# Attention's products of weights and values, both lanes side by side on TensorE: a change to the order of issue

## The chip, the cores and the metric

The kernel runs on one core of a Trainium2 chip. Five engines work side by side, each through its own instructions in a fixed order: TensorE (PE in the profile, with its weight loads as PEld), VectorE (DVE), ScalarE (ACT), GpSimd (POOL) and SyncE (SP), which here only starts transfers. The metric is the device time of one execution in microseconds (us), the median of several runs.

## The reference, cut to what matters

Two layers over 1024 latent and 256 context tokens, each with three token mixers (attention, a depthwise convolution, a Hyena long convolution), an output projection and an expert layer. The change lies in attention:

```
s = (jnp.einsum('bqhd,bkhd->bhqk', qn, k_nope, ...)
     + jnp.einsum('bqhr,bkr->bhqk', qr, k_rope, ...))
w = jax.nn.softmax(s * scale, axis=-1).astype(v.dtype)
return jnp.einsum('bhqk,bkhd->bqhd', w, v)
```

There are 8 heads. A latent query reads all 1280 keys, a context query the 256 context keys; scores contract over 96 numbers, and a head's value has 64 columns.

## The kernel before

Python code records the instructions, and a scheduler then sets each engine's order from priorities (the order of recording, unless a context says otherwise) and from its own model of the durations. What comes out is fixed at build time, so an instruction that waits holds up everything behind it on its engine.

`mla` (L595) records the attention of one layer. The work of a head is cut into units: one tile of 128 keys (kt) for two lanes of queries. For latent tokens the lanes are the two halves (512 queries each) of one head; in the first layer there are also units whose lanes are two heads' 256 context queries. A layer has 80 latent units, and the first layer 8 context units besides, so 168 units in all, with two products of weights and values each: 336.

A unit (`attend`, L772) does this for each lane. `score` (L783) multiplies keys by queries in three products, high and low parts apart (`mm3`, L93, hence lines L95 to L97), into one of the two PSUM banks tagged "s"; ScalarE takes the exponential (L788) into a tile `pt`, of which there are six. `pv` (L790) multiplies the values Vt (128 keys by 64 columns) by pt, in plain float32 through `mm` (L99, the line L100 of the profile), into PSUM tile `o`: lane 0 into partitions 0 to 63, lane 1 into 64 to 127 of the same bank. GpSimd adds each pt to a running sum (L801), from which the denominators come later (`finish`, L809: the products `p<-psum,ones`, a reciprocal on VectorE).

The loop at L672 records for unit n: the scores of unit n+1 for lane 0, a step of the next head's preparation, the scores of lane 1, another step, then `pv` of unit n, and another step. The preparation of the next head (`queries`, `keys`, `largest`) contains 24 or more products `p<-K,Q` (L757), each of which VectorE reduces to a maximum (L758) out of one of three banks "p". The long convolutions (`hyena`) are recorded within head 0 and are spread by the scheduler over the following heads. Their blocks go round: products `hx` on TensorE, two multiplications on VectorE (L862, L863), two additions on GpSimd (L864, L865), a split into two parts on ScalarE and VectorE (L90, L91), products `ha` on TensorE, each with one PSUM bank.

Of the kernel before, what the change touches and what calls it, by code (L numbers as in the profile page):

```python
# [29 lines left out]
def _bc(ap, n):  # L30
    """A DRAM row read by n partitions."""
    return bass.AP(tensor=ap.tensor, offset=ap.offset, ap=[[0, n]] + [list(x) for x in ap.ap])


def lap(parts):
    """The steps of parts one after another; what a part has left after it yields 1 alternates with the next one's first steps."""
    before = iter(())
    for part in parts:
        for late in part:
            yield  # L40
            if next(before, None):
                yield
            if late:
                break
        for _ in before:
            yield
        before = part
    for _ in before:
        yield


class Kernel:
# [9 lines left out]
    def stream(self, l, i):  # L62
        """128 tokens behind a layer's attention, or behind all of it."""
        return self.xd[l][128 * i:128 * i + 128] if i < 8 else self.xc[128 * (i - 8):128 * (i - 8) + 128]
# [5 lines left out]
    def banks(self, es, **tags):  # L70
        """PSUM banks for a part of the program, so many for each use."""
# [30 lines left out]
    def rsqrt(self, out, ss):  # L102
        """(ss + eps) ** -0.5 of a few columns."""
        n = out.shape[-1]
# [4 lines left out]
    def consts(self):  # L109
        nc, A, cp = self.nc, self.A, self.cp  # L110
# [16 lines left out]
        # the mixers' outputs: heads but the last two, the last two, the channels  # L127
# [6 lines left out]
    def mod(self, l, P, ps):  # L134
        """Two of the six rows at a time; yields between loads."""
# [31 lines left out]
    def sin(self, P, out, x, n):  # L167
        """sin of [128, n] of any size: x - 2 pi round(x / 2 pi) in parts."""
# [14 lines left out]
    def filter_mlp(self, F, P, PL, ps, taps):  # L183
        """The filter networks' last hidden layers, 64 partitions for each network, and what else the taps need."""
# [22 lines left out]
        for k, w in enumerate((w1, w2)):  # L207
# [8 lines left out]
            if k:  # L216
                # the sum and the difference of the two directions' weights, with zeros for the other network
# [9 lines left out]
    def filter_taps(self, l, F, P, ps, f):  # L227
        """Sums and differences of the two directions' taps, and the sums of their squares (twice the taps')."""
# [6 lines left out]
        for i in range(nts):  # L235
# [7 lines left out]
            if i in (0, 8):  # L243
                # no backward tap at zero
# [14 lines left out]
    def spectra(self, pools, PF, ps, jobs, lo_t, nk, units, mats, er_, n, nrm_i):  # L259
        """jobs: (taps, DRAM of the spectra); the transforms' matrices are read once for all. Pools for each job; the  # L260
        last one's is everybody's, and may come after the first yield. PF: for what is to be split."""
# [25 lines left out]
        def norms(f, rsr):  # L287
            """Two steps: the sums over the positions, then their roots as a row for all partitions."""
# [20 lines left out]
        for nm, s_, op in kinds:  # L309
            dat += [operands((nm, s_, op), ji) for ji in range(len(dat), len(J))]  # L310
            for un, ex, m, kind, unit in units:
# [15 lines left out]
                if roots:  # L327
                    # not before the first products
# [19 lines left out]
    def filters(self):  # L348
        A = self.A
        with ExitStack() as es:  # L350
# [11 lines left out]
            # kinds: real, imaginary, and the first unit's real part for the sines  # L362
# [34 lines left out]
    def win(self, l, M):  # L397
# [3 lines left out]
        with ExitStack() as es:  # L401
# [3 lines left out]
            with ExitStack() as es2:  # L405
                # first what comes before the products
# [23 lines left out]
                for g0, g1 in ((0, 4), (4, 8), (8, 10)):  # L430
# [27 lines left out]
                    # q, kv, k_rope  # L458
# [107 lines left out]
    def conv(self, l, M, P, ps):  # L566
        """Layer norm over the channels, silu."""
# [27 lines left out]
    def mla(self, l, M):  # L595
        """Attention, with the convolution's norm and the long convolutions in between: one order of TensorE's work."""
        nc, A, S, V, G = self.nc, self.A, self.S, self.V, self.G
        last = l == 1
        with ExitStack() as es:
# [13 lines left out]
            def fixed(i):  # L613
                """The rows that all heads share."""
# [12 lines left out]
            def values(i):  # L627
                """V of four heads, by tokens."""
# [12 lines left out]
            def prepare(h):  # L641
                """A head's keys and queries, and the queries' largest scores, by steps."""
# [29 lines left out]
            for h, w in enumerate(windows):  # L672
                # the next head's steps between this one's tiles of keys
# [35 lines left out]
    def queries(self, P, ps, l, h, M, Q, QC, tab):  # L709
        """A head's queries."""  # L710
# [27 lines left out]
    def keys(self, P, ps, l, h, M, K):  # L738
        """A head's keys."""
# [8 lines left out]
    def largest(self, P, ps, K, Q, nq, k0, nk, first):  # L748
        """The negated largest score of each query, into its row 96."""
# [22 lines left out]
    def attend(self, P, ps, l, lanes, Vt, kts):  # L772
        """Two lanes (head, keys, queries, the first of so many queries, their place) side by side, by tiles of keys."""
# [5 lines left out]
        def unit(n, kt):  # L779
# [3 lines left out]
            def score(i):  # L783
                _, K, Q, c, _, _ = lanes[i]
                p = ps("s")
                self.mm3(p[:, :N], K[0][:, s], K[1][:, s], Q[0][:, c:c + N], Q[1][:, c:c + N], True, True)
# [3 lines left out]
            def pv():  # L790
                if n == 0:
                    st.o = ps("o")
                for i, pt in enumerate(u.pts):
                    c = 64 * (lanes[i][0] % 4)
                    self.mm(st.o[64 * i:64 * i + 64, :N], Vt[kt][:, c:c + 64], pt[:, :N], n == 0, kt == kts[-1])
# [29 lines left out]
    def heads(self, l, h, M):  # L825
        """The weights of a head's keys and queries."""
# [6 lines left out]
    def hyena(self, l, M, P, ps):  # L833
        """Yields where other work may come first."""
# [11 lines left out]
        def table(src):  # L846
            """A matrix in two parts, each [128, a, b]."""
# [8 lines left out]
        def product(px, gt, u, w, y):  # L856
            """(Xc | Xs) in PSUM times the filter's spectrum (real, imaginary), in two parts."""
# [19 lines left out]
        def halves(o, blk):  # L877
            """Even and odd parts, folded once more: one block of their transforms, and back."""
# [52 lines left out]
        def whole(o, ct, D):  # L931
            """The odd multiples, the sum, and the gate."""
# [39 lines left out]
        def context(o):  # L972
            T = self.t(P, [128, 2, 2, 256], F32R, "hT", bufs=2)
            # C2 S2 C4 and S4 C2i S2i
# [22 lines left out]
            for u, ic, is_ in ((0, 4, 5), (1, 2, 3)):  # L997
                yh, yl = y[u]
                # the even unit's cosines and the odd unit's sines are symmetric
# [19 lines left out]
        def parts(o):  # L1019
            # halves folded about their middles; the operands of the sines of odd multiples (e, oe) run backwards, by which  # L1020
            # their transform is the cosines' up to signs, which the spectra carry
# [17 lines left out]
    def wout(self, l, R):  # L1039
# [4 lines left out]
        with ExitStack() as es:  # L1044
            # first the places that attention leaves early
# [30 lines left out]
            def source(n):  # L1076
                """n columns of the mixers' outputs: the last heads' part comes last."""
# [36 lines left out]
            def channels(i):  # L1114
                """The convolutions' part of a tile of tokens."""
# [14 lines left out]
            def heads(i):  # L1130
                """The heads' part, the residual, norm 2, and the router."""
# [73 lines left out]
    def affinities(self, R, s):  # L1205
        """Softmax over the experts (s: 0 latent, 1 context)."""
# [13 lines left out]
    def selected(self, R, s):  # L1220
        """The right-hand sides of the compaction: token, token, affinity in two parts."""
# [8 lines left out]
    def route_ctx(self, R, ps, ar, wk):  # L1230
        """Each expert's tokens of the context: the places of the 32 largest."""
# [19 lines left out]
    def route(self, R, ps, tag, P):  # L1251
        """Each expert's 128 tokens: rows of 128 affinities (tile of tokens, expert) are sorted and merged by twos to the 128th largest."""
# [5 lines left out]
        def merge(x, y, out, n, steps):  # L1258
            """n rows of bitonic sequences, descending."""
# [9 lines left out]
        for r in range(8):  # L1269
            # two halves in turns  # L1270
# [8 lines left out]
        for n in (64, 32):  # L1279
            # the 128 largest of two sorted rows, and those sorted  # L1280
# [10 lines left out]
        # all above the 128th largest, and the first of those equal to it  # L1291
# [22 lines left out]
    def moe(self, l, R):  # L1314
        nc, A, S, V, G = self.nc, self.A, self.S, self.V, self.G
        last = l == 1
        with ExitStack() as es:
            PA = self.pool(es, f"moa{l}", 1)
            if last:
                PM = self.pool(es, f"mob{l}", 1)  # L1320
                # the output projection leaves this place first
# [3 lines left out]
                # where nothing of the output projection's is  # L1325
# [10 lines left out]
            def fetch(e):  # L1336
                """The expert's tokens and gates; its tokens' rows."""
# [41 lines left out]
            def tokens(e):  # L1379
                """Its tokens, features by partitions."""  # L1380
# [28 lines left out]
            def weights(nm, e, kh, after=None):  # L1409
                w = large()  # L1410
                if after is not None:
                    # the load follows what is in the queue already
                    V.tensor_copy(w[:, 0, 0:1], after)
# [3 lines left out]
            def product(w, kh, x, accs, early=0):  # L1417
                """accs += x's tokens by half of the rows."""
# [12 lines left out]
            def up(e, kh, m):  # L1431
# [7 lines left out]
                # the first parts while VectorE chooses  # L1439
# [77 lines left out]
            def norm(x, g):  # L1517
                """The final norm of 128 tokens in place."""
# [5 lines left out]
            def final():  # L1524
                """All tokens as though the last expert had none, then its own."""
# [15 lines left out]
            # the first expert's weights come in while the experts choose  # L1541
# [9 lines left out]
            for e in range(17):  # L1551
                if e == 0:
                    # not before what the choice waits for
# [34 lines left out]
    def run(self, stop=None):  # L1588
# [9 lines left out]
        for l in range(2):  # L1598
            # the second layer's from the other end: what the first leaves early comes first
            self.side = ("left", "right")[l]  # L1600
            with ExitStack() as es:
                MP = self.pool(es, f"mix{l}", 1)
                # first what is in use until the end
# [12 lines left out]
            with ExitStack() as es:  # L1616
# [3 lines left out]
                # sums over an expert's rows, all and earlier ones  # L1620
# [12 lines left out]
def _r12(a):  # L1633
    """float64 -> the nearest float32 with 12 significant bits."""
# [10 lines left out]
def _mat(a):  # L1645
    """[t, f] -> [128, 2, t / 128, f]: both parts, rows by partition."""
# [4 lines left out]
def _constants():  # L1651
# [14 lines left out]
    # rotary tables  # L1666
# [131 lines left out]
```

## Time and profile before

| | us |
|---|---|
| median of 3 runs (lowest, highest) | 3534.89 (3531.77, 3535.91) |
| profiled execution, its span from the first to the last instruction | 3541.2 |
| TensorE busy in it | 3291.5 (93%) |
| VectorE, ScalarE, GpSimd busy | 2533.4 (72%), 1692.6 (48%), 1296.5 (37%) |
| attention of the first layer, from 540 to 1040 | 500 |
| attention of the second layer, from 2265 to 2755 | 490 |

The profile gives no time of the profiled execution other than its span, which is 6.3 us above the median of the runs. How to read it: a product in plain float32 is recorded as two MATMULs with a weight load each, so that the 336 products of weights and values are 672 records. Ends of matmuls are modelled and overlap the next one's start; what a product costs TensorE is therefore read from start to start. "128*64 128x512" is a matmul with 128 rows and 64 columns of weights and 512 columns streamed.

### The profile page before, as it was taken

The numbers are of one execution on the slowest core, as the hardware profiler recorded it, in microseconds if no ns is written. First come the engines' busy times: TensorE is split into PE (matmuls) and PEld (weight loads), VectorE is DVE, ScalarE is ACT, GpSimd is POOL, SyncE is SP. The second block draws the span as 40 slices with busy tenths as digits, with TensorE's granted clock in tenths as the row PEclk, the third lists the DMA queues.
The fourth block names the chain that finished last, engine by engine and source line by source line (L and its number), as shares of the span: only waits on it lengthen the run. The fifth ranks groups of instructions, "written<-read, shape, count | busy, mean of one in ns | idle before, by whom it ended". The sixth has DMA issues, their size and how long they took to land. (4 is left out here: it accounts for less than half of the span.)

```text
span 3541.2 us, 42696 instructions
## 1 busy us (share of the span) xinstructions
PE 3291.5 (93%) x15595; PEld 2244.1 (63%) x15595; DVE 2533.4 (72%) x3507; ACT 1692.6 (48%) x2447; POOL 1296.5 (37%) x1130
## 2 busy tenths in 40 slices
PE   8898989999999699999999879899999959999996
PEld 2467864566448566766767567646554647888885
DVE  7744796676557767777777556966663668999886
ACT  4214334333433256556665443433333426777775
POOL 4421434644553421112211113464455423343334
PEclk9898989999999799999999989899999979999998
DMA  8871121131234467777777611211222457999994
GB/s 314 309 248 62 38 90 40 49 93 47 60 113 140 158 253 276 297 276 282 295 271 297 211 59 54 84 50 49 67 73 80 155 220 289 374 382 378 373 380 181
DMA packets 138075, 660.80 MB, mean 187 GB/s; under 512 B 20520, under 2 KB 58824, under 8 KB 107145
## 3 DMA queue, kind: packets, MB, share of 16 engines
q1 hardware_dynamic: 112681, 582.85, 43.8%
q0 software_dynamic: 24768, 74.05, 7.6%
q8 instruction: 123, 2.02, 0.2%
q10 hardware_dynamic: 416, 1.18, 0.1%
q14 instruction: 87, 0.71, 0.1%
HBM read 589.24 MB, written 68.78 MB: 186 GB/s over the span
## 5 line engine op out<-in xcount | busy, mean ns | idle before, releaser
L91 DVE TENSOR_TENSOR mwl<-raw,mwh 128x1024 fp32r<-128x1024 f32 x710 | 881.2, 1277 | 225.4 <-ACT mwh L90 215.8
L90 ACT ACTIVATE mwh<-raw 128x1024 fp32r<-128x1024 f32 x768 | 791.1, 1057 | 353.4 <-PE acc L97 117.5
L96 PE MATMUL acc<-mwl,xh 128*128 128x512 f32 x1024 | 406.5, 397 | 0.5 <-DVE mwl L91 0.5
L97 PE MATMUL acc<-mwh,xl 128*128 128x512 f32 x1024 | 404.1, 396 | 0.1
L801 POOL TENSOR_TENSOR psum<-psum,pt 128x512 f32<-128x512 f32 x252 | 328.6, 1312 | 185.7 <-ACT pt L788 179.7
L788 ACT ACTIVATE pt<-s 128x512 f32<-128x512 f32 (+1 forms) x336 | 196.6, 586 | 390.8 <-PE s L97 363.5
L95 PE MATMUL acc<-mwh,xh 128*128 128x512 f32 x1024 | 373.9, 402 | 6.3 <-ACT xh L90 5.9
L100 PE MATMUL o<-pt,Vt 128*64 128x512 f32 (+1 forms) x672 | 338.9, 607 | 0.4 <-ACT ao L805 0.3
L758 DVE TENSOR_REDUCE mx<-p 128x1 f32<-128x512 f32 (+1 forms) x374 | 209.0, 587 | 153.4 <-PE p L100 152.6
L1498 POOL DMA_INDIRECT xd<-ymoe,idx x31 | 104.4, 3367 | 549.2 <-DVE ymoe L1494 472.6
L95 PEld LDWEIGHTS acc<-mwh,xh 128*128 128x128 f32 x1024 | 192.7, 190 | 69.4 <-ACT mwh L90 10.5
L96 PEld LDWEIGHTS acc<-mwl,xh 128*128 128x128 f32 x1024 | 194.1, 190 | 44.5 <-DVE mwl L91 2.6
L97 PEld LDWEIGHTS acc<-mwh,xl 128*128 128x128 f32 x1024 | 193.4, 190 | 40.1 <-issue 0.8
L91 POOL TENSOR_TENSOR mwl<-raw,mwh 128x1024 fp32r<-128x1024 f32 x58 | 150.4, 2598 | 185.2 <-ACT mwh L90 121.5
L564 DVE SCALAR_TENSOR_TENSOR cacc<-pad,cw,cacc 128x1295 f32<-128x1295 f32 (+1 forms) x90 | 165.7, 1841 | 1.3
L97 PE MATMUL mm<-hTh,wfl 128*128 128x512 f32 (+1 forms) x400 | 151.2, 379 | 12.7 <-DVE wfl L91 12.7
L95 PE MATMUL mm<-hTh,wfh 128*128 128x512 f32 (+1 forms) x400 | 152.5, 381 | 4.0 <-ACT wfh L90 4.0
L96 PE MATMUL mm<-hTl,wfh 128*128 128x512 f32 (+1 forms) x400 | 152.0, 380 | 0.0
L562 POOL TENSOR_TENSOR cacc<-cacc,tap 128x1295 f32<-128x1295 f32 (+1 forms) x30 | 97.0, 3233 | 120.8 <-ACT tap L561 118.6
L100 PEld LDWEIGHTS o<-pt,Vt 128*64 128x64 f32 x672 | 62.0, 134 | 110.2 <-issue 104.2
L100 PE MATMUL cx<-raw,xcT 128*32 128x512 f32 x1024 | 122.9, 597 | 0.0
L95 PE MATMUL mm<-woh,yhh 128*128 128x512 f32 x280 | 115.7, 416 | 6.0 <-ACT wt L1126 3.9
(539 smaller groups left out, 7322.4 us busy)
## 6 DMA issues: line engine op xcount, KB each, us to landing
raw<-in_w_gate_dram SPq DMA_DIRECT2D x64, 2048.0 KB
raw<-in_w_up_dram SPq DMA_DIRECT2D x64, 2048.0 KB
raw<-in_w_down_dram SPq DMA_DIRECT2D x64, 2048.0 KB
mw<-in_mod_w_dram SPq DMA_DIRECT2D x48, 1024.0 KB
ht<-in_k_C_dram POOLq DMA_DIRECT2D x24, 512.0 KB, 4.9
wfr<-in_w_fm_dram SPq DMA_DIRECT2D x20, 512.0 KB
hd<-h SPq DMA_DIRECT2D x18, 512.0 KB
fw<-in_k_filt_dram POOLq DMA_DIRECT2D x17, 512.0 KB, 6.2
```

Of the source, the lines that this page charges most:

```text
L90: self.S.activation(hi, src, AF.Copy)
L91: (eng or self.V).tensor_tensor(lo, src, hi.bitcast(F32), ALU.subtract)
L95: mm(out, ah, bh, start=first, stop=False, skip_group_check=True)
L96: mm(out, ah, bl, start=False, stop=False, skip_group_check=True)
L97: return mm(out, al, bh, start=False, stop=last, skip_group_check=True)
L100: return self.T.matmul(out, a, b, start=first, stop=last, skip_group_check=True)
L562: G.tensor_tensor(a, a, t, ALU.add)
L564: V.scalar_tensor_tensor(a, x, w2[:, ct, k:k + 1], a, ALU.mult, ALU.add)
L758: V.tensor_reduce(mx[:, q, n:n + 1], p[:, :N], AX.X, ALU.max)
L788: S.activation(pt[:, :N], p[:, :N], AF.Exp, scale=ATT_SCALE)
L801: (V if tail and n > 8 else G).tensor_tensor(sm[:, :N], st.sums[i][:, :N], pt[:, :N], ALU.add)
L1498: G.indirect_dma_start(self.xd[l], bass.IndirectOffsetOnAxis(ap=d["idx"], axis=0), y, None, compute_op=ALU.add)
```

## The change

In `pv` the two products are recorded under a higher priority, and are not to be issued before the last product that the latest `score` recorded, which is lane 1 of the next unit. `score` keeps that product for it. Nothing is added or removed; what is computed stays the same. The diff also drops comments and docstrings of the whole file, which do not reach the program, and lines behind L794 move by two (L801 becomes L803, for instance).

```
             def score(i):
                 _, K, Q, c, _, _ = lanes[i]
                 p = ps("s")
-                self.mm3(p[:, :N], K[0][:, s], K[1][:, s], Q[0][:, c:c + N], Q[1][:, c:c + N], True, True)
+                self.scored = self.mm3(p[:, :N], K[0][:, s], K[1][:, s], Q[0][:, c:c + N], Q[1][:, c:c + N], True, True)
                 pt = u.pts[i] = self.t(P, [128, 512], F32, "pt", bufs=6)
                 S.activation(pt[:, :N], p[:, :N], AF.Exp, scale=ATT_SCALE)
 
             def pv():
                 if n == 0:
                     st.o = ps("o")
-                for i, pt in enumerate(u.pts):
-                    c = 64 * (lanes[i][0] % 4)
-                    self.mm(st.o[64 * i:64 * i + 64, :N], Vt[kt][:, c:c + 64], pt[:, :N], n == 0, kt == kts[-1])
+                with self.tc.high_priority(400), self.tc.issue_after(self.scored.ins):
+                    for i, pt in enumerate(u.pts):
+                        c = 64 * (lanes[i][0] % 4)
+                        self.mm(st.o[64 * i:64 * i + 64, :N], Vt[kt][:, c:c + 64], pt[:, :N], n == 0, kt == kts[-1])
```

The first place is TensorE in the middle of the second layer's seventh head, before the change. Here s are scores, o the products of weights and values (two lanes of one tile have the same Vt), p the next head's products for the largest scores.

```order
L95 MATMUL s_21512<-Q0h_17870,K0h_17872 128x512
L96 MATMUL s_21512<-Q0l_17871,K0h_17872 128x512
L97 MATMUL s_21512<-Q0h_17870,K0l_17873 128x512
L100 MATMUL o_21351<-pt_21491,Vt_4560_20567 64x512
L100 MATMUL p_21453<-K1h_17876,Q1h_17874 128x512
L100 MATMUL p_21456<-K1h_17876,Q1h_17874 128x512
L95 MATMUL s_21524<-Q0h_17870,K0h_17872 128x512
L96 MATMUL s_21524<-Q0l_17871,K0h_17872 128x512
L97 MATMUL s_21524<-Q0h_17870,K0l_17873 128x512
L100 MATMUL o_21351<-pt_21500,Vt_4560_20567 64x512
```

The same place after the change:

```order
L95 MATMUL s_21512<-Q0h_17870,K0h_17872 128x512
L96 MATMUL s_21512<-Q0l_17871,K0h_17872 128x512
L97 MATMUL s_21512<-Q0h_17870,K0l_17873 128x512
L95 MATMUL s_21524<-Q0h_17870,K0h_17872 128x512
L96 MATMUL s_21524<-Q0l_17871,K0h_17872 128x512
L97 MATMUL s_21524<-Q0h_17870,K0l_17873 128x512
L100 MATMUL o_21351<-pt_21491,Vt_4560_20567 64x512
L100 MATMUL o_21351<-pt_21500,Vt_4560_20567 64x512
L100 MATMUL p_21465<-K1h_17876,Q1h_17874 128x512
L100 MATMUL p_21474<-K1h_17876,Q1h_17874 128x512
```

The o of lane 0 has moved behind the scores of the next tile's lane 1 and stands beside the o of lane 1; p products follow the pair or stand between the two lanes' scores.

The second place is TensorE at the first unit of the first layer, before the change. hx and ha here are transposes of the convolutions.

```order
L97 MATMUL s_3849<-Q0h_3582,K0l_3585 128x512
L100 MATMUL o_3918<-pt_3841,Vt_681_3683 64x512
L586 MATMUL hx_4267<-ident_60,m1y_4265 128x128 x2
L574 MATMUL ha_4277<-ident_60,cacc_1771 128x128 x2
L95 MATMUL s_3903<-Q0h_3582,K0h_3584 128x512
L96 MATMUL s_3903<-Q0l_3583,K0h_3584 128x512
L97 MATMUL s_3903<-Q0h_3582,K0l_3585 128x512
L100 MATMUL o_3918<-pt_3847,Vt_681_3683 64x512
```

The same place after the change:

```order
L97 MATMUL s_3849<-Q0h_3582,K0l_3585 128x512
L586 MATMUL hx_4267<-ident_60,m1y_4265 128x128 x2
L574 MATMUL ha_4277<-ident_60,cacc_1771 128x128 x2
L95 MATMUL s_3903<-Q0h_3582,K0h_3584 128x512
L96 MATMUL s_3903<-Q0l_3583,K0h_3584 128x512
L97 MATMUL s_3903<-Q0h_3582,K0l_3585 128x512
L100 MATMUL o_3918<-pt_3841,Vt_681_3683 64x512
L100 MATMUL o_3918<-pt_3847,Vt_681_3683 64x512
```

The convolutions' instructions now follow the scores directly, with no o ahead of them. Over the whole program TensorE's order before has 293 products of 512 columns that stand alone, 12 pairs and one row of three; after, 8 alone and 156 pairs (four of them as two rows of four). Of the 16 products of 256 columns, all stood alone; after, 4 do, and 6 pairs. On the other engines 515 of 3356 rows of VectorE, 388 of 2352 of ScalarE, 99 of 1131 of GpSimd and 19 of 640 of SyncE change their place, all of them in the two attention stages or at their edges; the other stages keep their order.

## Rows read from the trace of the kernel before

**Rows 1.** Busy time of the engines in four stretches: us, busy (count), PEclk.

```profile
core 0: us, PE busy (x) PEld busy (x) DVE busy (x) ACT busy (x) POOL busy (x), PEclk, DMA share, GB/s
540.00:1040.00 500.00, 489.48 (x2015) 266.95 (x2015) 318.19 (x527) 189.01 (x366) 262.96 (x255) 1.00 0.21 59
2040.00:2265.00 225.00, 194.54 (x859) 157.33 (x859) 159.15 (x200) 90.94 (x157) 67.63 (x59) 0.91 0.17 55
2265.00:2755.00 490.00, 480.83 (x1874) 257.51 (x1871) 302.43 (x494) 181.34 (x347) 260.10 (x254) 0.99 0.22 67
```

**Rows 2.** Groups by line, 540 to 1040: count, busy, mean ns, idle before it and releasers.

```profile
L801 POOL TENSOR_TENSOR psum<-psum,pt 128x512 f32<-128x512 f32 x126 | 164.7, 1316 | 87.3 <-ACT pt L788 82.4 <-DVE wql L91 3.4
L758 DVE TENSOR_REDUCE mx<-p 128x1 f32<-128x512 f32 (+1 forms) x182 | 100.9, 580 | 84.3 <-PE p L100 83.8
L788 ACT ACTIVATE pt<-s 128x512 f32<-128x512 f32 (+1 forms) x172 | 98.7, 577 | 190.9 <-PE s L97 171.8 <-PE o L100 15.4 <-POOL psum L801 2.6
```

**Rows 3.** The products o: all records of the tile.

```profile
L100 PE MATMUL o<-pt,Vt x672: 379/593/644, 534.5 to 2751.9; 128*64 128x512 f32 x160, 128*64 128x256 f32 x8
```

**Rows 4.** TensorE in order of time, second layer's last head: start, us, what.

```profile
2728.88 0.50 PE L95 MATMUL s<-Q1h,K1h 128*128 128x512 f32 x1
2729.22 0.39 PE L96 MATMUL s<-Q1l,K1h 128*128 128x512 f32 x1
2729.45 0.40 PE L97 MATMUL s<-Q1h,K1l 128*128 128x512 f32 x1
2729.77 1.07 PE L100 MATMUL o<-pt,Vt 128*64 128x512 f32 x2
2730.78 0.50 PE L95 MATMUL s<-Q1h,K1h 128*128 128x512 f32 x1
```

**Rows 5.** TensorE in order of time, where two o stand next to each other.

```profile
2567.61 0.39 PE L96 MATMUL s<-Q0l,K0h 128*128 128x512 f32 x1
2567.85 0.39 PE L97 MATMUL s<-Q0h,K0l 128*128 128x512 f32 x1
2568.16 1.08 PE L100 MATMUL o<-pt,Vt 128*64 128x512 f32 x4
2569.17 0.39 PE L95 MATMUL hx<-hT,ht 128*128 128x256 f32 x1
2569.40 0.28 PE L96 MATMUL hx<-hT,ht 128*128 128x256 f32 x1
2569.51 0.28 PE L97 MATMUL hx<-hT,ht 128*128 128x256 f32 x1
```

**Rows 6.** TensorE in order of time, an o of 256 columns.

```profile
1000.33 0.65 PE L100 MATMUL o<-pt,Vt 128*64 128x256 f32 x2
1000.91 0.50 PE L95 MATMUL s<-Q1h,K1h 128*128 128x512 f32 x1
1001.25 0.39 PE L96 MATMUL s<-Q1l,K1h 128*128 128x512 f32 x1
```

**Rows 7.** Weight loads at the pair of rows 5, and single ones by line, 2265 to 2755.

```profile
2568.16 0.20 PEld L100 LDWEIGHTS o<-pt,Vt 128*64 128x64 f32 x4 [0.36 <-issue]
...
L100 PEld LDWEIGHTS o<-pt,Vt 128*64 128x64 f32 x320 | 29.7, 134 | 53.7 <-issue 52.4 <-ACT pt L788 0.2
```

**Rows 8.** Stretches of 25 us in which VectorE is fullest.

```profile
590.00:615.00 25.00, 24.62 (x84) 10.62 (x83) 21.17 (x36) 10.73 (x21) 8.73 (x7) 1.00 0.18 48
2340.00:2365.00 25.00, 25.00 (x92) 11.80 (x91) 22.61 (x34) 11.05 (x21) 14.04 (x11) 1.00 0.14 39
```

**Rows 9.** The convolutions' additions on GpSimd by line, 540 to 1040, then 2265 to 2755.

```profile
L864 POOL TENSOR_TENSOR m1y<-m1y,m2y 128x128 f32<-128x128 f32 (+1 forms) x28 | 19.0, 678 | 52.0 <-DVE m2y L863 44.9 <-DVE m L761 4.2 <-ACT Q1h L769 1.9
...
L864 POOL TENSOR_TENSOR m1y<-m1y,m2y 128x128 f32<-128x128 f32 (+1 forms) x24 | 13.4, 559 | 47.7 <-DVE m2y L863 45.0 <-DVE m L762 2.5
```

**Rows 10.** GpSimd's sums in the last head, in order of time.

```profile
2728.79 1.28 POOL L801 TENSOR_TENSOR psum<-psum,pt 128x512 f32<-128x512 f32 x1 [0.61 <-ACT pt L788]
2730.68 1.28 POOL L801 TENSOR_TENSOR psum<-psum,pt 128x512 f32<-128x512 f32 x1 [0.61 <-ACT pt L788]
```

## The prediction

> **What bounds the kernel now.** I read first the busy time by stage. In the two attention stages, 990 us together, TensorE is busy 489.48 of 500 and 480.83 of 490 us, at a granted clock of 1.00 and 0.99, while VectorE has 318.19 and 302.43, GpSimd 262.96 and 260.10, ScalarE 189.01 and 181.34 us [rows 1]. The groups by line then say whom the others wait for: VectorE's maxima stand idle 83.8 us for TensorE's p, ScalarE's exponentials 171.8 us for the scores, and GpSimd's sums 82.4 us for those exponentials [rows 2]. So everybody waits for TensorE, and a microsecond less of work there is a microsecond less of time until another engine, or a round trip through several, comes to the front. The other stages keep their order, and I leave them as they are.
>
> Busy time of TensorE has modelled, overlapping ends, so next I read starts in order of time. In the last head, where nothing stands between, one lane takes 2730.78 - 2728.88 = 1.90 us: three scores and one o [rows 4]. Scores follow each other at 0.235 us (2567.61 to 2567.85 [rows 5], 2729.22 to 2729.45 [rows 4]), so three are 0.705 and one lone o costs 1.90 - 0.705 = 1.19 us: 1.01 until the next product starts, some 0.09 more ahead of it (0.32 from the last score, not 0.235), and 0.10 behind it (the first score after it takes 0.34).
>
> **What a pair costs.** The kernel before has a few places where the two lanes' products already stand next to each other, and one of them shows the price. From the last score at 2567.85 to the second hx at 2569.40 are 1.55 us [rows 5]. The score's own 0.235 and one hx of 256 columns at 0.12 (2569.40 to 2569.51, rounded) off, the block of two products, four records, is 1.19 us: as much as one alone. The two lanes write different halves of the partitions and run at the same time. The trace has 11 such rows of four, the first at 594.5 and the last at 2708.4, all with 1.01 us from their first start to the next product's; this one stands for them.
>
> **A rule against it.** The row shows four weight loads in 0.20 us, 0.13 us each when alone [rows 7], so those of lane 1 are hidden beside those of lane 0. The Trainium skill, page "TensorE: Matmul & The Clock Gate", section "Part 3: Packing small matmuls — row/col tiling", says that a weight load overlaps products in flight only when the row group differs; here the two lanes share all rows and differ in columns, so by that rule the second lane's two loads of 0.134 us would be exposed. Here the trace disagrees with it. What that would make of the time is a rival below, with a small chance.
>
> **The change part by part.** It adds and removes no instruction. (1) *Products of 512 columns.* In the order before, 293 stand alone, 12 in pairs and three in a row, which is 293 + 12 + 2 = 307 slots for the 320 products; after, 8 alone and 156 pairs are 164 slots. 143 slots fewer at 1.19 us: 170.2 us. (2) *Products of 256 columns.* 16 slots become 10. One costs 0.58 us until the next start (1000.33 to 1000.91), and with the same 0.19 around it 0.77 [rows 6]: 6 x 0.77 = 4.6 us. Together 336 products are in the order, twice as many records in the trace [rows 3]. TensorE's work in the two stages falls by 175 us, from 990 to 815.
>
> (3) *The wait that is added.* The pair waits for the scores of the next unit. Behind it on TensorE stand p, hx and the following scores. The wait for its own exponentials costs nothing: the scores ahead of the pair go into the two "s" banks, which are free only once both exponentials of the pair's own tile are done, so TensorE can't reach the pair earlier than its data. The price moves to the scores, which need those banks. A unit of the last head would take TensorE 2 x 0.705 + 1.19 = 2.60 us, and an exponential 0.58 to 0.60 [rows 2]; from the end of a lane's scores to the same bank's next use lie a pair and the other lane's scores, 1.9 us, against one exponential with its hand-over, or two when they queue (1.2 us). I cost it at nothing; that cover is gone only where ScalarE stands more than 0.7 us behind.
>
> (4) *GpSimd's sums and the six pt.* A sum is 1.28 us [rows 10], two per unit 2.56. Against 1.90 us per lane now, GpSimd waits 0.61 each time; in the last heads it comes just level with TensorE's 2.60 and its slack is gone. Per stage it has 263 of 408 us. Bounds: 0, and 10 us for the two ends together (two heads of 10 units at up to 0.5 us each); I take 3.
>
> (5) *VectorE.* Its 621 us are 63% of 990 and 76% of 815. In its fullest stretches it has 21.2 and 22.6 of 25 us [rows 8]. A stretch of 25 us holds some 4 merged pairs, 5 us, so TensorE would want 20, and these two lose 1.2 and 2.6 us. Bounds: 0, and 15 for four times that in shorter bursts; I take 6.
>
> (6) *The convolutions' round trips.* hx, VectorE, GpSimd, ScalarE, VectorE, ha: 28 and 24 blocks [rows 9]. Where the fixed order puts a block's next product just in time, TensorE now reaches it too early, by 1.19 us for each merged pair between. Bounds: 0, where a block's slack holds it, and 52 x 1.19 = 62 us, where each block shows one pair's worth. GpSimd's waits of 44.9 and 45.0 us for VectorE within these blocks [rows 9] say that the path is long, but TensorE is almost never idle for it now. I take a third of the bound, 0.33 x 62 = 20 us, nearer to the row without stalls. (7) *Transfers.* SyncE's and GpSimd's queues keep nearly all their places, and the transfers use 0.21 and 0.22 of their engines in these stages [rows 1]: nothing.
>
> Sum: 170.2 + 4.6 - 3 - 6 - 20 = 146 us. The profiled execution's span of 3541.2 becomes 3395; it lies 6.3 us above the median of the runs, so the median of 3534.89 becomes 3389.
>
> **The rivals.** *Round trips come to light.* VectorE and the convolutions' blocks are late at nearly every turn: 62 + 15 + 10 = 87 us of the 175 are given back, and the time is 3535 - 88 = 3447 at its worst, about 3425 in its middle (110 us saved). For it speaks VectorE at 76%; against it, that it waits 83.8 us for TensorE in one stage alone [rows 2]. With it goes the clock: in the stretch before the second attention TensorE is busy 194.54 of 225 us and the clock is granted at 0.91, where attention has 1.00 [rows 1], so stalls on TensorE could cost more than their own length. *Only the products overlap.* By the rule on weight loads a pair costs 2 x 0.134 = 0.27 us more; 143 x 0.27 = 38 us less gain, 3427. Rows 5 and 7 speak against it, eleven times. *No pairing in time.* If lane 1's product, though next in the queue, started a slot later, nothing would be gained: 3535. Step 3 says why its operand is there. *Slower: the scores wait for the exponentials.* Two lanes' scores in a row take both banks at once. If ScalarE, which also splits the heads' keys and queries, were late by one slot in each unit, each of 168 units would lose 1.19 us, 200 us against the 175 gained: 3560. It decides from 175 / 168 = 1.04 us per unit. Against it: ScalarE is busy 38% of the stage, and exponentials wait for scores 171.8 us, not the other way [rows 2].
>
> **How the numbers follow.** The forecast, with part of the cover gone: chance 0.66, 3389, its own range 3362 to 3412. Round trips come to light: 0.24, 3412 to 3447. Weight loads exposed: 0.04, 3427. No cover needed at all, or a little more than 175 us gained because today's few stalls go as well: 0.02, 3355. No pairing in time: 0.02, 3535. Slower: 0.02, 3560. The range that holds 8 in 10 is 3358 to 3434. A measurement of this kernel can tell about 0.2%, 7 us, from no change. Faster has 0.66 + 0.24 + 0.04 + 0.02 = 0.96, same 0.02, slower 0.02.
>
> **What would show it.** In the profile after, o stands in rows of four records with some 1.08 us, about 160 of them, and a unit of the last head repeats every 2.6 us, not 3.8. The two attention stages last about 990 - 146 = 844 us with the granted clock still near 1.0, VectorE's share is near 74%, and the idle time of the maxima and of the exponentials behind TensorE has shrunk. The second rival shows as idle time of TensorE ahead of hx, ha or p with VectorE or ScalarE as releaser, and as a granted clock under 0.97. The prediction is wrong if rows of four take clearly over 1.1 us, if scores wait for exponentials at most units, or if a stage outside attention moves by over 10 us.

## The result, and the profile after

The changed kernel takes 3404.98 us (median of 4 runs, 3398.4 to 3407.12), the kernel before 3534.01; the ratio is 0.9629 (95% interval 0.9615 to 0.9643). That is 131 us less by the ratio, 129 by the two medians. In a later comparison it was 0.9624 (0.9608 to 0.964), 133 us less by both. The forecast was 3389, with a range from 3358 to 3434.

The two attention stages by engine, after the change. The first one again begins at 540; the second is taken 28 us ahead of its first o and to 3 us behind its last, as in [rows 1].

```profile
core 0: us, PE busy (x) PEld busy (x) DVE busy (x) ACT busy (x) POOL busy (x), PEclk, DMA share, GB/s
540.00:970.00 430.00, 409.83 (x2002) 259.49 (x2001) 311.27 (x524) 186.82 (x363) 259.05 (x252) 0.98 0.24 69
2192.00:2617.00 425.00, 405.04 (x1871) 255.03 (x1871) 302.94 (x493) 179.85 (x345) 263.94 (x253) 0.96 0.25 78
```

They last 855 us instead of 990: 135 us less, all of the result within its uncertainty. Three things are to be read against [rows 1]. TensorE is not busy for 20.17 + 19.96 = 40.1 us, where it was 10.52 + 9.17 = 19.7. The granted clock is 0.98 and 0.96, where it was 1.00 and 0.99. The other engines do the same work in less time; VectorE's share is 72%.

TensorE in the last head, in order of time, answers to [rows 4]:

```profile
2604.47 0.40 PE L97 MATMUL s<-Q1h,K1l 128*128 128x512 f32 x1
2604.79 1.08 PE L100 MATMUL o<-pt,Vt 128*64 128x512 f32 x4
2605.80 0.50 PE L95 MATMUL s<-Q1h,K1h 128*128 128x512 f32 x1
...
2607.09 0.39 PE L97 MATMUL s<-Q1h,K1l 128*128 128x512 f32 x1
2607.40 1.08 PE L100 MATMUL o<-pt,Vt 128*64 128x512 f32 x4
2608.41 0.50 PE L95 MATMUL s<-Q1h,K1h 128*128 128x512 f32 x1
```

The pair of four records takes 1.01 us until the next product's start, and a unit 2607.40 - 2604.79 = 2.61 us, where two lanes took 3.80. Among the single records behind such a row of four, lane 1's products start less than 0.01 us behind lane 0's: the two lanes do run at the same time. The weight loads at one such pair, and the products' records as a whole, answer to [rows 7] and [rows 3]:

```profile
2604.79 0.20 PEld L100 LDWEIGHTS o<-pt,Vt 128*64 128x64 f32 x4 [0.37 <-issue]
...
L100 PE MATMUL o<-pt,Vt x672: 379/593/1116, 534.2 to 2614.0; 128*64 128x512 f32 x160, 128*64 128x256 f32 x8
```

The median is the same 593 ns; the longest is 1116 where it was 644: records of that kind stand where the clock was lower, as seen below. The groups by line, from 540 to 970, answer to [rows 2]:

```profile
L803 POOL TENSOR_TENSOR psum<-psum,pt 128x512 f32<-128x512 f32 x126 | 165.2, 1330 | 32.6 <-ACT pt L788 30.6
L758 DVE TENSOR_REDUCE mx<-p 128x1 f32<-128x512 f32 (+1 forms) x182 | 98.4, 577 | 38.5 <-PE p L100 38.1
L788 ACT ACTIVATE pt<-s 128x512 f32<-128x512 f32 (+1 forms) x170 | 97.1, 577 | 129.9 <-PE s L97 96.5 <-PE o L100 17.9 <-POOL psum L803 12.4
```

Everybody still waits mostly for TensorE, but less: the maxima 38.1 us where it was 83.8. The 12.4 us behind GpSimd's sums (2.6 before) are new. In the last head GpSimd's sums stand without a gap, where [rows 10] had 0.61 us between them:

```profile
2601.20 7.69 POOL L803 TENSOR_TENSOR psum<-psum,pt 128x512 f32<-128x512 f32 x6
```

What TensorE waits for in the first attention stage (us in total, times, longest):

```profile
PE p L768 <- DVE m L762: 9.2, 6, 2.4
PE hx L95 <- DVE m2y L865: 3.9, 4, 1.6
PE hx L900 <- DVE hT L91: 3.8, 2, 3.5
PE ha L97 <- DVE yl L91: 0.9, 1, 0.9
```

L768 are the transposes of the negated maxima (m), which close a head's preparation; the others are the convolutions' blocks. All four wait for VectorE. One of these waits in order of time:

```profile
736.34 1.06 PE L900 MATMUL hx<-ident,cacc 128*128 128x128 f32 x4 [3.47 <-DVE hT L91]
737.05 0.78 PE L95 MATMUL s<-Q1h,K1h 128*128 128x512 f32 x1
737.62 0.63 PE L96 MATMUL s<-Q1l,K1h 128*128 128x512 f32 x1
738.05 0.63 PE L97 MATMUL s<-Q1h,K1l 128*128 128x512 f32 x1
738.61 1.64 PE L100 MATMUL o<-pt,Vt 128*64 128x512 f32 x4
```

and the engines around it by stretch, columns as above:

```profile
725.00:735.00 10.00, 7.76 (x34) 3.96 (x32) 10.00 (x18) 3.92 (x8) 5.30 (x5) 1.00 0.36 94
735.00:740.00 5.00, 3.67 (x11) 1.85 (x11) 5.00 (x6) 0.60 (x1) 3.00 (x3) 0.66 0.00 0
740.00:765.00 25.00, 24.50 (x146) 17.98 (x145) 17.26 (x32) 10.54 (x22) 18.50 (x18) 1.00 0.36 95
```

VectorE is busy all the time from 725 to 740. TensorE stands idle for 3.47 us, and then the granted clock goes to 0.66 on the average of 5 us: for part of it the lower of the two levels, 1.2 GHz. Scores start 0.43 us apart instead of 0.235, and a pair is recorded with 1.64 us instead of 1.08. So this wait is paid for twice. Behind the first o of each layer the changed kernel has nine waits of 1.5 us or more. During seven of them, or soon after, the lower level comes; at two, of 1.60 and 1.67 us, it does not, and an eighth stretch at the lower level follows waits of 0.21 and 0.47 us only. In the profile of the second measurement one more wait, of 1.94 us, is not followed by it. The kernel before has one such stretch there, behind waits of 1.23 and 0.47 us.

### The profile page after: what moved, and what is told of

It reads as the page before. It is cut to its first block, busy times and chain, and to the rows that moved or that the text cites. A ratio compares the mean times of both kernels' runs of the same rounds, so it can differ in the third digit from the quotient of the medians.

```text
span 3396.6 us, 42699 instructions
## 1 busy us (share of the span) xinstructions
PE 3126.6 (92%) x15595; PEld 2226.8 (66%) x15595; DVE 2532.4 (75%) x3507; ACT 1691.3 (50%) x2447; POOL 1300.8 (38%) x1130
## 5 line engine op out<-in xcount | busy, mean ns | idle before, releaser
L803 POOL TENSOR_TENSOR psum<-psum,pt 128x512 f32<-128x512 f32 x252 | 333.1, 1341 | 68.3 <-ACT pt L788 64.4
L100 PE MATMUL o<-pt,Vt 128*64 128x512 f32 (+1 forms) x672 | 184.1, 611 | 0.0
L96 PE MATMUL mm<-wol,yhh 128*128 128x512 f32 x280 | 112.1, 401 | 0.0
```

The source lines that it names most:

```text
L96: mm(out, ah, bl, start=False, stop=False, skip_group_check=True)
L100: return self.T.matmul(out, a, b, start=first, stop=last, skip_group_check=True)
L803: (V if tail and n > 8 else G).tensor_tensor(sm[:, :N], st.sums[i][:, :N], pt[:, :N], ALU.add)
```

## Experiments

"Idle" below is the time in which TensorE is not busy in the two attention stages, and "clock" is what the granted clock costs there: (1 - granted clock) times the time, added up over short stretches, since two digits over a whole stage leave some 2 us open. Of the clock's cost some 7 us lie ahead of the second layer's first o in the kernel before, and as many in the changed kernel; what falls into idle time (2 us in the changed kernel) counts in both. Stages are taken as above, from 5 or 6 us behind the first o in the first layer and from 27 to 30 us ahead of it in the second, to 3 to 5 us behind the last.

### Priority without the bond

```
-                with self.tc.high_priority(400), self.tc.issue_after(self.scored.ins):
+                with self.tc.high_priority(400):
```

> The two products of a tile keep their higher priority but not the bond to the next tile's last score. In TensorE's order 285 products of 512 columns then stand alone again (8 in the changed kernel) and 18 pairs are left. Theory (the gain comes from two lanes' products standing next to each other): the time is that of the kernel before, 3534 us, within 15. Rival (the gain comes from the priority, which makes the scheduler lay the rest of attention better): about 3405 us, as with the whole change.

Measured: 3531.38 us, ratio 0.9987 (0.9977 to 0.9997). The stages:

```profile
540.00:1040.00 500.00, 490.62 (x2021) 271.11 (x2020) 317.74 (x527) 189.44 (x367) 260.08 (x255) 1.00 0.20 59
2262.00:2752.00 490.00, 480.72 (x1874) 263.03 (x1872) 300.45 (x494) 180.70 (x347) 260.15 (x254) 0.98 0.22 68
```

They are as long as before, 990 us. The theory's time came. The priority alone does nothing that counts; with the bond to the next tile's last score (`issue_after`) come the pairs, since lane 0's product then can't be laid as soon as its pt is ready. Whether the bond would do without the priority was not run.

### Pairs in one half of the partitions

```
-                        self.mm(st.o[64 * i:64 * i + 64, :N], Vt[kt][:, c:c + 64], pt[:, :N], n == 0, kt == kts[-1])
+                        h = 64 * i if n == 0 else 0
+                        self.mm(st.o[h:h + 64, :N], Vt[kt][:, c:c + 64], pt[:, :N], n == 0, kt == kts[-1])
```

> The changed kernel, but from each window's second tile of keys on both lanes' products go into partitions 0 to 63 of the bank (lane 1's share of the output is left out, its products are still made). Order and pairs are nearly the same: some 150 pairs, about 145 of them in one half. Theory (two products overlap because they use different halves): each such pair costs some 0.97 us more, and only the 0.2 us around a block is still shared: 3490 to 3520 us, with about 2.0 us from a pair's first start to the next product. Rival (what is saved is the change between 64 and 128 columns around each block, or better order): 3400 to 3415 us.

Measured: 3508.42 us, ratio 0.9924 (0.9904 to 0.9944), as the theory had it. The stages, and TensorE in the last head:

```profile
543.00:1032.00 489.00, 468.54 (x2008) 280.19 (x2007) 311.80 (x524) 187.01 (x363) 255.62 (x253) 0.98 0.20 60
2256.00:2730.00 474.00, 457.53 (x1876) 269.93 (x1874) 292.35 (x495) 181.63 (x348) 259.42 (x254) 0.97 0.23 71
```

```profile
2702.66 0.40 PE L97 MATMUL s<-Q1h,K1l 128*128 128x512 f32 x1
2702.98 1.93 PE L100 MATMUL o<-pt,Vt 128*64 128x512 f32 x4
2704.84 0.50 PE L95 MATMUL s<-Q1h,K1h 128*128 128x512 f32 x1
...
2706.43 1.93 PE L100 MATMUL o<-pt,Vt 128*64 128x512 f32 x4
```

The same four records take 1.86 us where they took 1.01, now one behind the other, 0.43 to 0.48 us apart. A unit takes 2706.43 - 2702.98 = 3.45 us, against 2.61 with the overlap and 3.80 before. The trace has 128 such rows, and 128 x 0.85 = 109 us; the stages are 963 - 855 = 108 us longer, and the kernel gives back 103 us. So the larger part of the gain, about four fifths, is the overlap of two lanes in different halves, and not the order. (In one half both lanes also add into the same addresses of the bank. A run with the same half of two banks, which would tell this from the half as such, was not made.)

The rest, 27 us against the kernel before, is what standing together is worth besides. A pair in one half costs 1.86 + 0.19 = 2.05, two lone products 2 x 1.19 = 2.38; some 130 times 0.33 are 43 us, and the 20 or so pairs that stay in two halves (11 before) add some 10. Idle and clock take part of it back (36.9 and 24 us here, 19.7 and 9 before).

What these 0.19 us at the edges of a block are, one place of the kernel before narrows down. The products `p<-kvh,wkh` have 64 columns of weights, but come in high and low parts, as the scores do:

```profile
2340.79 0.39 PE L97 MATMUL s<-Q1h,K1l 128*128 128x512 f32 x1
2341.02 0.39 PE L95 MATMUL p<-kvh,wkh 128*64 128x512 f32 x1
...
2341.47 0.39 PE L97 MATMUL p<-kvh,wkl 128*64 128x512 f32 x1
2341.70 0.39 PE L95 MATMUL s<-Q1h,K1h 128*128 128x512 f32 x1
...
2342.17 0.39 PE L97 MATMUL s<-Q1h,K1l 128*128 128x512 f32 x1
2342.49 1.07 PE L100 MATMUL o<-pt,Vt 128*64 128x512 f32 x2
```

From 128 columns to 64 and back they follow at 0.23 us, like scores among themselves; o, also of 64 columns, comes only 0.32 us behind a score. So the change between 64 and 128 columns, of which the rival above speaks, does not make this edge by itself. It goes with products that are in plain float32 as well, as o's are; why was not tested.

### VectorE relieved

```
-                V.tensor_reduce(mx[:, q, n:n + 1], p[:, :N], AX.X, ALU.max)
+                V.tensor_reduce(mx[:, q, n:n + 1], p[:, :N // 2], AX.X, ALU.max)
...
-        self.negated = V.tensor_scalar(m1[:, :qt], m1[:, :qt], -1.0, None, ALU.mult)
+        self.negated = V.tensor_scalar(m1[:, :qt], m1[:, :qt], -1.0, -500.0, ALU.mult, ALU.add)
```

In the changed kernel:

> The changed kernel with VectorE's maxima taken over half of each chunk of scores (and an offset of -500 on the negated maximum; the maximum is no longer the true one). This takes about 0.26 us off 248 reductions and 0.13 off 126, some 80 us of VectorE's work in the two attention stages. Theory A (of the 175 us less of TensorE's work some 40 did not arrive, and most of them are TensorE waiting for a VectorE that is fuller now): 15 to 25 us faster than the changed kernel, 3380 to 3390. Theory B (they are the length of the convolutions' round trips, or the clock, and not VectorE's load): within 6 us of 3405.

and in the kernel before:

> The kernel before with the same halved maxima and offset. Both theories: TensorE bounds it and hardly waits for VectorE, so 0 to 8 us faster than 3534. If it gains 15 us or more, VectorE's load already cost that much before, and a gain of the changed kernel with halved maxima says nothing of the change.

Measured: 3366.29 us, ratio 0.9519 (0.9503 to 0.9535), and 3510.25 us, ratio 0.9928 (0.9911 to 0.9944). The changed kernel gains 39 us by it, more than both theories had it, but the kernel before gains 25, and by what was written ahead of the run the first number alone then says nothing of the change. The stages of the relieved changed kernel, and then those of the relieved kernel before:

```profile
538.00:962.00 424.00, 406.33 (x2010) 258.62 (x2009) 277.93 (x528) 186.43 (x366) 259.65 (x254) 0.98 0.24 70
2174.00:2585.00 411.00, 394.02 (x1884) 248.42 (x1884) 260.04 (x505) 180.91 (x350) 266.25 (x256) 0.99 0.26 82
```

```profile
535.00:1028.00 493.00, 486.61 (x2014) 264.62 (x2013) 279.06 (x530) 189.43 (x368) 260.24 (x255) 1.00 0.20 60
2242.00:2726.00 484.00, 473.25 (x1884) 256.17 (x1884) 260.24 (x507) 182.72 (x351) 263.65 (x256) 0.99 0.22 70
```

The stages shrink from 855 to 835 and from 990 to 977 us, so the change is worth 142 us with a relieved VectorE and 135 without: VectorE's load as such takes 7 us of what did not arrive. By the medians it is 11 to 15: 3510.25 - 3366.29 = 144 us with a relieved VectorE, 129 to 133 without. Of the rest of what both kernels gained, some 10 us lie between the first layer's last o and the second layer's first, in which the second layer's first maxima fall. Idle falls only from 40.1 to 34.7 us, although VectorE has 76 us less to do. So most of TensorE's idle time does not come from how much VectorE has to do in all; that VectorE gets to the right piece late is the likely reading, which no run here shows.

### The kernel once more, and earlier preparation

> The changed kernel once more, beside the two that follow. Both theories: 3405 us within 5, ratio 0.962 to 0.965.

Measured: 3402.03 us, ratio 0.9624 (0.9608 to 0.964). Beside it:

```
-SLACK, DEN = (4, 4), (2, 2)
+SLACK, DEN = (10, 10), (2, 2)
```

> The changed kernel with SLACK 10 in place of 4: the steps that prepare the next head are laid so that they are done 10 slots (3.3 units) before the head's end, not 4. In the changed kernel some 13 of 36 us that TensorE stands idle in attention lie ahead of the transposes of the negated maxima, which a head's last p products and their reductions precede at once. Theory A (these waits, and the clock that falls after some of them, are part of what did not arrive): idle time ahead of these transposes under 6 us, 5 to 15 us faster than the changed kernel. Theory B (the waits move to the convolutions' products, or VectorE's load sets them): within 4 us of it.

Measured: 3391.33 us, ratio 0.9598 (0.9585 to 0.9611), about 9 us faster by the ratios, 11 by the medians. The intervals overlap a little; the five runs of each kernel do not. Theory A's time came, but not by its mechanism: the idle time ahead of the transposes is 12.9 us, against 13.1, and idle as a whole 39.8 us instead of 40.1; the clock's cost is 19 instead of 26 (22 in the profile of the second measurement).

> The changed kernel with SLACK 14: the next head's steps are done 4.7 units before a head's end. With SLACK 10 the kernel took 3391 us, but its idle time ahead of the transposes stayed at 13 us. Theory A (earlier steps give the maxima more room, and the gain goes on): 3380 to 3389 us with under 10 us idle ahead of the transposes. Theory B (the gain with SLACK 10 is a matter of where the convolutions' products and the low clock happen to fall): 3388 to 3405 us, and the idle time in attention stays at 30 to 40 us.

Measured: 3397.92 us, ratio 0.9612 (0.9597 to 0.9627); idle 41.9, clock 24 us, 11.1 us idle ahead of the transposes. The time is theory B's, with idle 2 us above its range: more of the same does not go on. From SLACK 10 it can't be told apart, since the intervals overlap.

### Two banks for hx, two for p

```
-            ps = self.banks(es, s=2, o=1, p=3, hx=1, ha=1)
+            ps = self.banks(es, s=2, o=1, p=2, hx=2, ha=1)
```

> The changed kernel with two PSUM banks for the convolutions' products hx (one before) and two for p (three before). Theory A (the idle time ahead of hx and ha, some 16 us, comes from the one bank that VectorE must read before TensorE may write the next block): 5 to 12 us faster than the changed kernel. Theory B (it comes from the round trip through VectorE, GpSimd and ScalarE, which a second bank does not shorten, and p is short of a bank now): 0 to 15 us slower, with more idle time of TensorE ahead of p.

Measured: 3497.83 us, ratio 0.9891 (0.9876 to 0.9906), 96 us slower than the changed kernel, far outside both expectations. The stages, and what TensorE waits for in the first:

```profile
544.00:1031.00 487.00, 447.87 (x2007) 271.13 (x2008) 313.83 (x526) 187.60 (x362) 260.20 (x253) 0.92 0.21 61
2264.00:2725.00 461.00, 430.69 (x1862) 263.77 (x1861) 290.66 (x482) 178.48 (x339) 258.14 (x251) 0.92 0.23 71
```

```profile
PE p L100 <- DVE mx L758: 10.5, 31, 2.1
PE p L768 <- DVE m L762: 6.4, 7, 1.3
PE hx L900 <- DVE cacc L891: 5.1, 1, 5.1
```

The line of p in the second:

```profile
PE p L100 <- DVE mx L758: 15.4, 37, 3.2
```

Theory B is right on the cause, TensorE ahead of p (25.9 us in both stages here, 2.2 in the changed kernel), and wrong on the price. Idle rises from 40.1 to 39.1 + 30.3 = 69.4 us, 29 more, of which p takes 24. The clock goes to 0.92 and costs 78 us instead of 26, 52 more, though some 12 of the 78 fall into idle time. These two are most of the 93 us by which the stages are longer (948 instead of 855 us). The run changes both kinds of bank at once, and the kernel before was not run with two p banks, so what the third p bank is worth without the pairs is not shown.

### Later transposes

```
-        yield
+        for _ in range(4):
+            yield
         for c in range(0, nq, 512):
```

(with SLACK 10, and 36 and 44 steps of a head instead of 33 and 38)

> SLACK 10, and the transposes of the negated maxima recorded three steps (one unit) after these maxima. Theory A (TensorE waits there because nothing is queued between the maxima's products and the transposes): idle time ahead of the transposes falls from 13 to under 8 us, and the time to 3380 to 3389. Theory B (the scheduler puts them where it put them anyway): within 4 us of 3391.

Measured: 3387.89 us, ratio 0.9585 (0.9569 to 0.9601): 14 to 17 us faster than the changed kernel, but only 3 faster than SLACK 10 alone, with intervals that overlap. So most of the gain is that of SLACK 10. The time lies in the ranges of both theories; the idle time ahead of the transposes, 13.4 us, speaks for theory B. The stages are 840 us long, 15 less than in the changed kernel; idle is 35.6 and the clock 19 us, which accounts for 11 or 12 of the 15. The rest was not traced.

## Why the prediction was right, and where its sum was off

*TensorE bounds attention, and the rest of the kernel stays.* Right. The stages gave 135 us (844 us were forecast for them, 855 came), and the whole kernel 129 to 133.

*A pair costs as much as one product.* Right to the hundredth: 1.01 us to the next start and 2.61 per unit against 2.60 forecast. That the cause is the two halves was only argued from rows; the run with both products in one half shows that without them the overlap is gone. The weight loads of lane 1 stay hidden, four in 0.20 us, so the rival that exposed them is out; so are the rival without pairing, and the slower one, since TensorE's waits for exponentials ahead of scores stay under 2 us in all.

*175 us less work on TensorE.* It fits what the stages show, but only together with two losses: 135 us arrived, idle rose by 20.4 us and the clock's cost by some 17 (from 9 to 26), which makes 172. In the profile of the second measurement the clock's cost is 22, so it is good to a few us.

*The losses, 29 us in the sum (GpSimd 3, VectorE 6, round trips 20).* Their kind was right and their sum was mis-sized, because it lacks a term. Idle rose by 20.4, less than 29. Of it some 10 us lie ahead of hx and ha, forecast at 20, and 8 ahead of the transposes of the maxima, which the prediction did not name as a place. They are these lines, two of before and, with the 9.2 above, one of after:

```profile
PE p L768 <- DVE m L762: 3.2, 4, 1.1
PE p L768 <- DVE m L762: 1.4, 1, 1.4
PE p L768 <- DVE m L762: 3.9, 3, 1.6
```

The clock, 17 us, stood only in a rival, without a price. Step (6) counted a wait by its own length; here each microsecond of added idle time came with 0.8 more from the clock. With the measured losses the sum is 175 - 20 - 17 = 138, near the 135 of the stages. That the forecast missed by only 16 us is in part luck: the waits were put 9 us too high, which covers half of the clock that was left out. A sign of the rival in which round trips come to light did appear, a granted clock of 0.96 in the second stage where it named anything under 0.97, and so did its waits ahead of hx and ha; the time is still in the forecast's own range, near the rival's end of it.

*GpSimd level with TensorE in the last heads.* Right: its sums stand back to back, and a unit still takes 2.61. TensorE's waits for exponentials, through which a late GpSimd would reach it, are 1.4 us in both stages.

*From the span to the median.* The profiled executions differ by 3541.2 - 3396.6 = 145 us, the runs by 129 to 133, so the forecast of 146 looks better by the profiles than it was. Outside the two attention stages the profile after is 10 us shorter, but in the profile of its second measurement the span is 3400.8 and only some 2 us of that are left. These 10 us are a difference between executions, not the change.

What stays open is what sets the clock. Over the kernels run here its cost goes with idle only roughly, as the table shows: at about 40 us idle it is 19 to 26, at 35 to 37 it is 12 to 24.

| kernel | stages, us | idle, us | clock, us |
|---|---|---|---|
| before | 990 | 19.7 | 9 |
| priority only | 990 | 18.7 | 9 |
| changed | 855 | 40.1 | 26 |
| changed, second measurement | 852 | 40.4 | 22 |
| pairs in one half | 963 | 36.9 | 24 |
| relieved VectorE, changed | 835 | 34.7 | 12 |
| relieved VectorE, before | 977 | 17.1 | 3 |
| SLACK 10 | 848 | 39.8 | 19 |
| SLACK 14 | 853 | 41.9 | 24 |
| later transposes | 840 | 35.6 | 19 |
| two hx, two p banks | 948 | 69.4 | 78 |

## What to carry to other kernels

Where two products use different column halves of TensorE, look in the trace for places where they happen to stand together: their start-to-start time is the price of a pair, and here it was that of one product. A scheduler that lays each as soon as its data is there parted them here, and a dependency on something that comes later, with a priority, brought them together; the priority alone did not. When TensorE's work shrinks by a sixth, price each new wait on it at more than its length: against the kernel before, the clock added 0.5 to 0.9 us per us of idle time in most kernels here, and 1.4 in the run with fewer p banks. And count banks before trading them.

## What the runs showed of the hardware that had not been expected

Two plain float32 products of 64 columns (512 streamed) in the same half, next to each other, take 1.86 us to the next start, in two halves 1.01. About 0.19 us of each block stand at its edges, 0.09 ahead of it and 0.10 behind, so that two in one half cost 2.05 in all and two that stand apart 2 x 1.19 = 2.38. The 64 columns alone do not make these edges, since products in parts change between 64 and 128 columns at 0.23 us without one. One PSUM bank less for p and one more for hx cost 96 us, and about half of what the stages lost by it shows as a granted clock of 0.92 instead of 0.98 and 0.96.
